# Moving a per-layer embedding's projection to the front of a one-core decoder-layer kernel, with its norm applied at the last gate

## The chip, the cores and the metric

The kernel runs on one core of a Trainium2 chip. The metric is the device time of one execution in microseconds; each kernel is run several times and the median is compared. PE is the matrix engine (TensorE), DVE VectorE, ACT ScalarE, POOL GpSimd, and SP (SyncE) issues most DMAs.

## The reference

One decoder layer on 1024 tokens of width 1024, all in fp32. The part that the change touches is the per-layer embedding `e`; everything else comes before or after it.

```
u = rmsnorm(h, mix_norm_w); proj = u @ w_in             # gated DeltaNet and latent attention read proj
h = h + concat(y_gdn, y_mla) @ w_out
h = h + square(relu(rmsnorm(h, mlp_norm_w) @ w_up)) @ w_down
e = rmsnorm(p @ w_ple_proj, ple_post_norm_w)            # p: 1024 x 256, w_ple_proj: 256 x 1024
gate = sigmoid(rmsnorm(h, ple_gate_norm_w) @ w_ple_gate)
h = h + gate * e
return rmsnorm(h, final_norm_w)
```

`e` needs only `p` and weights, none of the layer's other results. It is used in the last step alone.

## The kernel before

The 1024 tokens are 8 blocks of 128 rows. Every fp32 product is three matmuls on fp32r halves (`three`, L212: hi by hi, hi by lo, lo by hi), so each operand is split into a high part (a cast on ACT) and a low part (a subtraction on DVE or POOL). A weight is loaded, cast and split by `load_rows` (L195 on).

The work up to the MLP is cut into named steps. The table `STEPS` (L65 to 92) lists their names in the order in which they are written out; a loop runs them. A scheduler then orders the instructions of each engine; it starts from that order. Each engine and each DMA queue goes through its instructions in order, so a DMA on SP's queue waits for those in front of it. SBUF is a set of 4 KB-a-row slots in five pools (`SLOTS`: u 16, m 8, g 14, w 7, r 3), and `HOMES` says from which pool a named tile takes its slot. PSUM banks are shared out by `TAGS`.

The steps at the front are:

- `ldx{b}` loads a block of x (512 KB, SP), `nx{b}` squares its rows (ACT), takes the root (POOL) and scales it (DVE, L175); `tx{g}_{k}` transposes the blocks of a token group (PE `pt_x`, L188) and splits them into `uT`.
- `ldm{k}` loads a quarter of the misc weights (the columns for gates and latents), `spm{k}` splits it into `mwh`, `mwl`; `misc{b}` multiplies one block by all four quarters, 24 matmuls into `acc_m` of 432 columns.
- `wl{m}` loads a column block of the input weights; `ip{m}` multiplies it (`acc_p`, L233 to 236). `ip4` is the first. It needs all of `uT`.

The embedding's steps are `plew` (loads the row of norm weights `rowp` and the weights `wp0`, `wp1`, and splits them), `ei{b}` (loads a 128 x 256 block of p into `et`, two transposes `pt_e`, split into `pthl`) and `eo{b}` (12 matmuls of 512 columns into two banks `pe`; per bank a copy on ACT to `et` and a Square on ACT whose sum goes to `se`; POOL makes the root; DVE scales by it and by `rowp`, L1218; SP stores the block to `ep_d`). They stand in the middle of the attention's steps (`s`, `v`, `ve` and others), between `vc0` and `s13`.

After the steps come the MLP's up and down stages, and the gate stage (L1541 to 1593). There `gate_in(b)` normalises block b of h by `norm_rows` (ACT, POOL, DVE) into `xg`, transposes it (`pt_g`) and splits it into `gh`, `gl`; it is called one block ahead. 48 matmuls `pgt` a block follow, the sigmoid `sg`, the product with `et` loaded from `ep_d`, the sum into `hb` and the final norm.

Of the kernel before, what the change touches and what calls it, by code (L numbers as in the profile page):

```python
# [70 lines left out]
sub sub0 ssq1_1 sub1 la11 sub2 sub3 sub4 sub5 sub6 sub7 sub8 sub9 xout ssq1_0 cv2 ssq2_1 wl8 wl9 ssq2_0 ip3 cv3 wl13
qout0 ip8 la10 cv8 rv0_0 rv0_1 kbd1_0 ga3 ga2 ssq3_0 qout1 wl11 ip9 cv9 kbd3_0 kbd2_0 tl0 kbd0_1 ga1 ga0 tm0 ip11
tn0 ip10 wl12 kbd1_1 rv1_0 tl1 tm1 kbd0_0 mw0 cv10 tl2 tl3 ip12 cv12 tn1 mw1 kbd3_1 kbd2_1 ssq3_1 rv2_0 rv1_1 tm2
tn2 cv11 ip13 cv13 rv3_1 tm3 tn3 mw2 mw3 rv3_0 mu0 sc0 rv2_1 mu3 mu1 wl15 mu2 sc1 sc2 sc3 wl14 ip15 qout2 ip14 cv14
la01 lt0_2 sc4 lt1_1 lt0_0 sc5 cv15 lt0_1 sc6 lt1_0 sc7 sc8 sc9 sc10 wv0 vb1 wpe qp0 vb0 qp1 sc11 vb3 rq8 vb2 lt1_2
rkey sc12 sc13 sc14 qout3 ol6 qp7 qr00 qp2 vb6 wn0 kn0_1 vb5 ol0 vb4 kn0_0 sc15 ol2 ol3 qn0_0 qp4 vb7 ol1 kp3 oa0
qp5 oa1 kp0 ob0 qp6 qp3 qn0_1 qr01 qr11 oa2 ro0_0 s0_1 qr10 s0_2 s0_3 ro0_1 s0_0 v0_0 v0_1 v0_2 s1_2 s1_0 s1_1 v0_3
ve0 s1_3 v1_0 v1_1 v1_2 v1_3 v1_4 kp1 s2_0 v1_5 kp2 v1_6 v1_7 ve1 ob1 ob2 s2_2 oa3 s2_1 ol4 oa4 ob3 s2_3 ob4 s3_1
ol5 s3_0 oa6 v2_0 s3_3 v2_1 v2_2 oa5 ob6 s3_2 v2_3 wn1 qn1_0 ro1_0 qn1_1 kn1_1 ve2 v3_0 v3_1 kn1_0 ro1_1 v3_2 v3_3
v3_4 s4_2 s4_1 fa0 ol7 s4_0 oa7 s5_2 s4_3 v3_5 v3_6 v3_7 ve3 v4_0 v4_1 v4_2 s5_1 fb0 s5_0 s6_2 s5_3 v4_3 ob5 s6_1  # L80
ve4 v5_0 kp5 s7_1 v5_1 v5_2 v5_3 v5_4 v5_5 v5_6 wv1 vc1 s6_3 ob7 ro2_0 s7_2 v5_7 s7_0 vc0 plew ei0 ei1 eo1 eo0 s6_0
h2 ve5 v6_0 v6_1 v6_2 wn2 kn2_0 v6_3 vc4 vc5 vc3 s7_3 vc7 ve6 v7_0 v7_1 v7_2 v7_3 qn2_0 vc6 vc2 v7_4 fa1 ei2 v7_5
qn2_1 kp4 s8_3 kn2_1 s8_1 eo2 ro2_1 v7_6 s8_2 s8_0 kp7 s9_3 s10_3 s9_1 s9_0 v7_7 ve7 v8_0 fb1 v8_1 v8_2 v8_3 s9_2
ve8 v9_0 v9_1 v9_2 v9_3 v9_4 ei3 s10_0 eo3 s10_2 s10_1 s11_1 s11_0 ei4 v9_5 v9_6 v9_7 ro3_0 ve9 s11_2 eo4 v10_0
v10_1 v10_2 v10_3 ve10 s11_3 ei5 ro3_1 eo5 wn3 qn3_0 kn3_0 v11_0 kn3_1 kp6 v11_1 v11_2 v11_3 v11_4 fa2 s12_2 qn3_1
# [1537 lines left out]
```

## Time and profile before

| | |
|---|---|
| time, three runs | 1462.49, 1461.21, 1453.26 us; median 1461.21 |
| profiled execution | 1459.25 us, of which 1457.5 are the span from the first to the last instruction |
| mean granted PE clock | 0.972 |
| busy share of the span | PE 95%, DVE 69%, ACT 45%, POOL 21% |
| first matmul of the input projection (`ip4`) | 69.38 us from the span's start |
| the embedding's steps | 485 to 612 us |
| gate stage | 1350 us to the end |

All durations come from the profiled execution; the times of the runs come without a profile. Rows give the engine, the line of the kernel, the operation and the tiles (out<-in, without buffer numbers). In rows by stretch the columns are the busy time and count of PE, PEld (weight loads), DVE, ACT and POOL, then PE's clock, the share of the DMA engines and GB/s.

### The profile page before, as it was taken

To read this page: it belongs to the slowest core of one execution; us is meant where nothing else is said; L and a number is where in the kernel's file an instruction comes from. 1 tells how busy PE (TensorE), PEld (TensorE's weight loads), DVE (VectorE), ACT (ScalarE), POOL (GpSimd) and SP (SyncE) were. 2 spreads that over 40 slices of the span, in tenths; PEclk is the share of its full clock that TensorE was granted. 3 is DMA by queue.
4 is the path that set the end of the run, shared out by engine and by line. 5 is a ranking of instruction groups with operands and counts; after the bars stand their busy time and mean duration, and the time that the engine had idled before them with its cause. 6 is when DMAs were issued, how large, how long until landed. Compare 5 with 4: busy or idle time off the path is not lost.

```text
span 1457.5 us, 22314 instructions
## 1 busy us (share of the span) xinstructions
PE 1380.4 (95%) x8575; PEld 1130.7 (78%) x8575; DVE 1007.5 (69%) x1617; ACT 662.8 (45%) x1169; POOL 307.4 (21%) x417
## 2 busy tenths in 40 slices
PE   5999968999899999999989999999999999999897
...
GB/s 214 49 54 59 131 58 130 85 81 86 59 66 65 140 82 106 152 196 130 88 66 151 159 159 159 159 137 125 214 333 230 159 96 126 183 116 134 170 44 58
DMA packets 133590, 182.54 MB, mean 125 GB/s; under 512 B 38896, under 2 KB 88188, under 8 KB 133484
## 3 DMA queue, kind: packets, MB, share of 16 engines
...
q10 hardware_dynamic: 160, 0.27, 0.0%
...
## 4 chain that ended last, share of the span: by engine, by line
PE 47%; DVE 11%; DMA 8%; ACT 6%; issue 3%; POOL 1%; SPq 1%; DVEq 0%; POOLq 0%; ACTq 0%
DMA i_d<-D 4%; PE dmo L214 3%; PE dme L214 3%; PE dmo L215 3%; PE dme L215 3%; PE dme L213 3%; PE dmo L213 3%; DMA dar<-i_d 2%; PE pgt L215 2%; PE pgt L213 2%; PE pgt L214 2%; PE um L215 2%; PE um L214 2%; PE um L213 2%; PE pt_p L1119 1%
## 5 line engine op out<-in xcount | busy, mean ns | idle before, releaser
L1495 DVE TENSOR_TENSOR dal<-dar,dah 128x1024 fp32r<-128x1024 f32 x56 | 68.5, 1224 | 74.4 <-issue 32.1
L1544 POOL DMA_DIRECT2D rowg<-in_ple_gate_norm_w x1 | 0.6, 644 | 505.4 <-DVE dbs L1499 505.4
L214 PE MATMUL dme<-dbl,dah 128*128 128x512 f32 x256 | 99.7, 390 | 0.0
L215 PE MATMUL dme<-dbh,dal 128*128 128x512 f32 x256 | 99.4, 390 | 0.0
L213 PE MATMUL dme<-dbh,dah 128*128 128x512 f32 x256 | 99.2, 390 | 0.0
L1494 ACT CAST dah<-dar 128x1024 fp32r<-128x1024 f32 x56 | 58.8, 1050 | 62.0 <-DMA dar<-i_d 59.5
L1501 ACT CAST dbh<-dbs 128x1024 fp32r<-128x1024 f32 x40 | 42.1, 1053 | 90.1 <-DVE dbs L1499 45.6
L214 PE MATMUL dmo<-dbl,dah 128*128 128x512 f32 x192 | 74.4, 390 | 1.8 <-DVE dbl L1502 1.8
L215 PE MATMUL dmo<-dbh,dal 128*128 128x512 f32 x192 | 74.3, 390 | 0.0
L213 PE MATMUL dmo<-dbh,dah 128*128 128x512 f32 x192 | 72.8, 390 | 0.0
L180 DVE TENSOR_TENSOR phl<-pt_p,phl 128x512 fp32r<-128x512 f32 (+1 forms) x96 | 51.8, 550 | 17.8 <-ACT phl L179 16.8
L1098 DVE TENSOR_REDUCE stat<-ps_s 128x1 f32<-128x384 f32 (+5 forms) x96 | 51.5, 551 | 16.4 <-PE ps_s L1097 9.7
L213 PEld LDWEIGHTS dme<-dbh,dah 128*128 128x128 f32 x256 | 48.1, 188 | 10.0
L214 PEld LDWEIGHTS dme<-dbl,dah 128*128 128x128 f32 x256 | 48.1, 188 | 9.9
L215 PEld LDWEIGHTS dme<-dbh,dal 128*128 128x128 f32 x256 | 48.1, 188 | 9.9
L213 PE MATMUL um<-uc,t52h 128*128 128x512 f32 x128 | 51.4, 402 | 3.5 <-DVE Cb L1420 2.7
L179 ACT CAST phl<-pt_p 128x512 fp32r<-128x512 f32 (+1 forms) x96 | 44.5, 480 | 21.9 <-PE pt_p L1119 19.5
L1502 DVE TENSOR_TENSOR dbl<-dbs,dbh 128x1024 fp32r<-128x1024 f32 x40 | 48.9, 1222 | 6.7 <-ACT dbh L1501 6.4
L214 PE MATMUL um<-uc,t52h 128*128 128x512 f32 x128 | 50.8, 397 | 2.6 <-DVE uc L1282 2.6
L214 PE MATMUL um<-uc,t34h 128*128 128x512 f32 x128 | 50.7, 396 | 0.7 <-DVE uc L1282 0.7
L213 PE MATMUL um<-uc,t34h 128*128 128x512 f32 x128 | 50.9, 398 | 0.0
L215 PE MATMUL um<-uc,t34l 128*128 128x512 f32 x128 | 50.4, 393 | 0.0
...
## 6 DMA issues: line engine op xcount, KB each, us to landing
dar<-i_d SPq DMA_DIRECT2D x56, 512.0 KB, 3.8
...
wu<-in_w_up SPq DMA_DIRECT2D x32, 512.0 KB, 4.7
x<-in_x SPq DMA_DIRECT2D x8, 512.0 KB, 9.8
h<-in_x SPq DMA_DIRECT2D x8, 512.0 KB, 4.5
ep_d<-et SPq DMA_DIRECT2D x8, 512.0 KB, 2.8
yr<-y_d SPq DMA_DIRECT2D x8, 512.0 KB, 5.8
h_d<-h SPq DMA_DIRECT2D x8, 512.0 KB, 2.6
```

The lines of the kernel that those rows point to most:

```text
L179: nc.scalar.copy(out=hi, in_=src)
L180: nc.vector.tensor_tensor(out=lo, in0=src, in1=f(hi), op=ALU.subtract)
L213: nc.tensor.matmul(outp, ah, bh, start=first, stop=False)
L214: nc.tensor.matmul(outp, ah, bl, start=False, stop=False)
L215: nc.tensor.matmul(outp, al, bh, start=False, stop=last)
L1098: nc.vector.tensor_reduce(out=st[:, c:c + 1], in_=ps[c], axis=AX.X, op=ALU.max, negate=True)
L1119: nc.tensor.transpose(pt[:, i * P:(i + 1) * P], pn_view(u, i)[:, kb * P:(kb + 1) * P], ident)
L1494: nc.scalar.copy(out=ah, in_=raw)
L1495: nc.vector.tensor_tensor(out=al, in0=raw, in1=f(ah), op=ALU.subtract)
L1501: nc.scalar.copy(out=bh, in_=s_)
L1502: nc.vector.tensor_tensor(out=bl, in0=s_, in1=f(bh), op=ALU.subtract)
L1544: nc.gpsimd.dma_start(out=rowg, in_=ple_gate_norm_w[0].partition_broadcast(P))
```

## The change

- `plew`, `ei{b}`, `eo{b}` move from the attention to the front of `STEPS`, among the loads of x and of the misc weights. The order of these front steps is another one too, and a few later steps change places (`la10`, `wl13`, `wl15`, `kp0`, `kp5`, `kp7`, `xout` and some near the end of the attention).
- p comes in two loads of four blocks each (`lp0`, `lp1`, new tiles `pb0`, `pb1`) in place of eight. Two blocks share a `pthl` tile.
- `eo{b}` stores the product as it is: one bank is copied by ACT, the other by DVE; the two Squares, the root and the scaling are gone. `ep_d` becomes eight tensors, one a block.
- In the gate stage, `gate_in(b)` loads the block of `ep_d`, and `norm_rows` normalises it with `rowp` into `en`. `rowp` is loaded at the start of this stage.
- Tiles change pools: the weights `wp0`, `wp1` to w, `pthl` to u, `x1`, `x2` to u.

```
-ldx0 ldm0 start ldx2 ldx1 ldx7 ldx3 ldm1 mixcol ldm2 nx0 nx1 ldm3 ldx5 tx0_3 nx2 nx3 tx0_7 ldx4 tx0_0 tx0_1 tx1_6
...
+lp0 ldx1 ldx0 plew start ei3 ei0 mixcol nx1 nx0 wl7 ei1 lp1 tx0_7 ei4 eo0
+wl5 ldm1 ldm0 ei2 spm1 eo1 tx0_0 ldx6 tx0_1 tx0_2 wl4 tx0_4 ldx3 masks ldx2 nx3
...
-    ep_d = dr.tile([T, D], F32, name="ep_d")
+    ep_d = [dr.tile([P, D], F32, name=f"ep_d{b}") for b in range(NB)]
...
     def _():
-        ple["row"] = slot("ple", "rowp")
-        nc.gpsimd.dma_start(out=ple["row"], in_=ple_post_norm_w[0].partition_broadcast(P))
         ple["w"] = [load_rows(w_ple_proj, k * P, f"wp{k}", ("plr", "ple", "ple")) for k in range(2)]

+    def ple_load(g):
+        nc.sync.dma_start(out=tile_(f"pb{g}", "pb").rearrange("q (b c) -> q b c", b=4),
+                          in_=p[g * 512:(g + 1) * 512].rearrange("(b q) c -> q b c", q=P))
...
     def ple_in(b):
-        pt_ = tile_(f"pthl{b}", "pth", F32R)
-        pb = tile_(f"et{b}", "et")[:, 0:256]
-        nc.sync.dma_start(out=pb, in_=p[b * P:(b + 1) * P])
-        transpose_split(pp_("pt_e"), [pb[:, 0:P], pb[:, P:2 * P]], pt_[:, 0:256], pt_[:, 256:512])
+        pb = tl[f"pb{b // 4}"][:, b % 4 * 256:(b % 4 + 1) * 256]
+        transpose_split(pp_("pt_e"), [pb[:, 0:P], pb[:, P:2 * P]], *ple_part(b))

     def ple_out(b):
...
-            nc.scalar.copy(out=et[:, hs], in_=pe2)
-            nc.scalar.activation(out=pe2, in_=pe2, func=AF.Square, accum_out=ss[:, h2:h2 + 1])
-        nc.gpsimd.tensor_tensor(out=ss[:, 2:3], in0=ss[:, 0:1], in1=ss[:, 1:2], op=ALU.add)
-        rsqrt_(ss[:, 3:4], ss[:, 2:3], 1.0 / D)
-        nc.vector.scalar_tensor_tensor(out=et, in0=et, scalar=ss[:, 3:4], in1=ple["row"], op0=ALU.mult, op1=ALU.mult)
-        nc.sync.dma_start(out=ep_d[b * P:(b + 1) * P], in_=et)
+            if h2:
+                nc.vector.tensor_copy(out=et[:, hs], in_=pe2)
+            else:
+                nc.scalar.copy(out=et[:, hs], in_=pe2)
+        nc.sync.dma_start(out=ep_d[b], in_=et)
...
+    rowg, rowf, rowp = slot("u", "rowg"), slot("u", "rowf"), slot("m", "rowp")
+    nc.gpsimd.dma_start(out=rowp, in_=ple_post_norm_w[0].partition_broadcast(P))
...
+        ep, et = slot("w", "et5"), slot("g", "en")
+        nc.sync.dma_start(out=ep, in_=ep_d[b])
+        norm_rows(ep, ste[:, b, 0:1], ste[:, b, 1:2], D, rowp, et)
+        return gh, gl, et
```

Three places show how the instructions stand. The first is SP's queue in the first tens of microseconds. Before, it begins with all of x and of the misc weights (`mwr`):

```order
L370 DMA x_128<-in_x 128x1024
L384 DMA mwr_130<-in_w_in 128x2x432
L370 DMA x_137<-in_x 128x1024
L370 DMA x_139<-in_x 128x1024
L370 DMA x_141<-in_x 128x1024
L370 DMA x_143<-in_x 128x1024
L384 DMA mwr_145<-in_w_in 128x2x432
```

In the changed kernel it begins with p and two blocks of x, and goes on like this, from the fourth DMA to the twentieth but one (x_270 is block 6, x_296 and x_317 are blocks 3 and 2, x_363 is block 5; ep_d_77, 78, 80 and 79 are blocks 0, 1, 3 and 2):

```order
L217 DMA w7r<-in_w_in 128x8x128
L395 DMA mwr_233<-in_w_in 128x2x432
L395 DMA mwr_235<-in_w_in 128x2x432
L1232 DMA ep_d_77<-et_209 128x1024
L217 DMA w5r<-in_w_in 128x8x128
L381 DMA x_270<-in_x 128x1024
L1232 DMA ep_d_78<-et_246 128x1024
L381 DMA x_296<-in_x 128x1024
L381 DMA x_317<-in_x 128x1024
L1232 DMA ep_d_80<-et_327 128x1024
L381 DMA x_363<-in_x 128x1024
L395 DMA mwr_375<-in_w_in 128x2x432
```

The loads of x3 and x2 now stand behind the stores of blocks 0 and 1 of the embedding, and that of x5 behind the store of block 3; the store of block 2 follows, and behind it `mwr_387`, x4 and x7.

The second place is PE's row in the front. Before, the misc matmuls of the first blocks begin right behind the transposes of x:

```order
L188 MATMUL pt_x<-ident,x_128 128x128
L188 MATMUL pt_x<-ident,x_139 128x128
L188 MATMUL pt_x<-ident,x_137 128x128
L188 MATMUL pt_x<-ident,x_143 128x128
L213 MATMUL acc_m<-mwh_249,uT_0_189 128x432
L214 MATMUL acc_m<-mwl_250,uT_0_189 128x432
L215 MATMUL acc_m<-mwh_249,uT_0_189 128x432
```

In the changed kernel the projection's blocks 0, 1, 3, 2 and half of 4 stand there with parts of the misc matmuls between them; this is the end of that piece, with the first transposes of x2 and x3 behind it:

```order
L226 MATMUL pe_405<-wp0h,pthl_204 128x512
L224 MATMUL pe_405<-wp1h,pthl_204 128x512
L225 MATMUL pe_405<-wp1l,pthl_204 128x512
L226 MATMUL pe_405<-wp1h,pthl_204 128x512
L199 MATMUL pt_e<-ident,pb_195 128x128 x2
L199 MATMUL pt_x<-ident,x_317 128x128
L199 MATMUL pt_x<-ident,x_296 128x128
L224 MATMUL acc_m<-mwh_365,uT_0_264 128x432
```

All 96 matmuls and 16 transposes of the projection now stand ahead of `ip4`; blocks 4 to 7 stand among the remaining transposes and misc matmuls.

The third place is PE in the attention, where block 1 of the projection stood before among the softmax's transposes (`pt_p`) and the values (`pv`):

```order
L214 MATMUL pv<-wv_5315,cT_0_3382 128x256
L215 MATMUL pv<-wv_5315,cT_0_3382 128x256
L1119 MATMUL pt_p<-ident,pn6a 128x128 x2
L1119 MATMUL pt_p<-ident,pn6b 128x128
L213 MATMUL pe_5435<-wp0h,pthl_5426 128x512
L214 MATMUL pe_5435<-wp0l,pthl_5426 128x512
L215 MATMUL pe_5435<-wp0h,pthl_5426 128x512
L213 MATMUL pe_5435<-wp1h,pthl_5426 128x512
```

In the changed kernel the rows of `pe` are gone from here, and the others follow each other.

More of the change, by code (lines that the diff above doesn't have):

```diff
@@ L71 @@
[L71 to L85, printed above, removed]
@@ new lines @@
+wl5 ldm1 ldm0 ei2 spm1 eo1 tx0_0 ldx6 tx0_1 tx0_2 wl4 tx0_4 ldx3 masks ldx2 nx3
+nx2 eo3 eo2 ldx5 spm0 tx0_6 ldm3 tx0_3 nx5 ldm2 ei5 ldx4 eo4 ldx7 eo5 tx1_7
+tx0_5 nx7 spm3 tx1_1 tx1_5 tx1_2 spm2 tx1_4 columns ei6 nx4 misc0 tx1_3 nx6 eo6 misc1
+tx1_0 tx1_6 tx2_0 tx2_3 misc3 tx2_1 tx2_5 tx2_6 ei7 tx2_2 misc2 eo7 tx2_4 tx2_7 misc5 misc7
+misc6 la00 misc4 ip4 cv4 gates wl6 ip5 cv5 ip7 wl0 ssk1_1 wl1 ssk0_1 ip6 cv7
+dec2 ssk1_0 dec1 ssk0_0 cv6 dec3 wl2 dec0 ssk3_0 ssk2_1 wl10 ssk2_0 gk1 ssk3_1 cvals ip1
@@ new lines @@
+rotary cv1 cunit ip0 cv0 gk0 ssq0_0 ssq0_1 uu1 ip2 gk2 uu2 gk3 uu0 uu3 wl3
+sub sub0 ssq1_1 sub1 la11 sub2 sub3 sub4 sub5 sub6 sub7 sub8 sub9 ssq1_0 cv2 la10
+ssq2_1 wl8 wl9 ssq2_0 wl13 ip3 cv3 xout qout0 ip8 cv8 rv0_0 rv0_1 kbd1_0 ga3 ga2
+ssq3_0 qout1 wl11 ip9 cv9 kbd3_0 kbd2_0 tl0 kbd0_1 ga1 ga0 tm0 ip11 tn0 ip10 kbd1_1
+wl12 wl15 tl1 tm1 cv10 kbd0_0 mw0 rv1_0 tl2 tl3 ip12 tn1 kbd3_1 ssq3_1 kbd2_1 cv12
+mw1 rv2_0 rv1_1 tm2 tn2 cv11 ip13 cv13 tm3 rv3_1 tn3 mw2 mw3 rv3_0 mu0 sc0
+rv2_1 mu3 mu1 mu2 qout2 sc1 sc2 wl14 ip14 ip15 sc3 cv14 la01 lt0_2 cv15 sc4
@@ new lines @@
+lt1_1 rq8 lt0_0 sc5 lt0_1 sc6 lt1_0 sc7 sc8 wv0 vb1 wpe qp0 sc9 vb0 qp1
+sc10 sc11 vb3 vb2 lt1_2 rkey sc12 sc13 qr00 sc14 qout3 ol6 qp7 qp2 vb6 wn0
+kn0_1 vb5 ol0 vb4 kn0_0 sc15 kp0 ol2 ol3 qn0_0 qp4 vb7 ol1 kp3 oa0 qp5
+oa1 ob0 qp6 qp3 qn0_1 qr01 qr11 qr10 ro0_0 s0_1 s0_2 oa2 s0_3 ro0_1 s0_0 v0_0
+v0_1 v0_2 s1_2 s1_0 s1_1 v0_3 ve0 s1_3 v1_0 v1_1 v1_2 v1_3 v1_4 kp1 s2_0 v1_5
+kp2 v1_6 v1_7 ve1 ob1 ob2 s2_2 s2_1 oa3 ol4 oa4 ob3 s2_3 ob4 s3_1 ol5
+s3_0 oa6 v2_0 oa5 v2_1 v2_2 s3_3 v2_3 wn1 ob6 s3_2 qn1_0 ro1_0 qn1_1 kn1_1 ve2
@@ new lines @@
+v3_0 v3_1 kn1_0 ro1_1 v3_2 v3_3 s4_2 s4_1 fa0 ol7 s4_0 v3_4 v3_5 oa7 s5_2 s4_3
+v3_6 v3_7 ve3 v4_0 v4_1 v4_2 s5_1 fb0 s5_0 s6_2 s5_3 kp5 v4_3 s6_1 ve4 v5_0
+ob5 s7_1 v5_1 v5_2 v5_3 v5_4 v5_5 v5_6 wv1 vc1 s6_3 ob7 ro2_0 s7_2 v5_7 s7_0
+vc0 s6_0 h2 ve5 v6_0 v6_1 v6_2 wn2 kn2_0 v6_3 vc4 kp7 vc5 vc3 s7_3 vc7
+ve6 v7_0 qn2_0 v7_1 v7_2 v7_3 vc6 fa1 v7_4 vc2 v7_5 qn2_1 kp4 s8_3 kn2_1 s8_1
+ro2_1 v7_6 s8_2 s8_0 s9_3 s10_3 s9_1 s9_0 v7_7 ve7 fb1 v8_0 v8_1 v8_2 v8_3 s9_2
+ve8 v9_0 v9_1 v9_2 v9_3 v9_4 s10_0 s10_2 s10_1 s11_1 s11_0 v9_5 v9_6 v9_7 ro3_0 ve9
@@ new lines @@
+s11_2 v10_0 v10_1 v10_2 v10_3 ve10 s11_3 wn3 qn3_0 ro3_1 kn3_0 v11_0 v11_1 v11_2 v11_3 v11_4
+fa2 v11_5 kn3_1 kp6 v11_6 v11_7 s12_2 qn3_1 s12_1 s12_0 y0 ve11 s12_3 v12_0 v12_1 v12_2
+v12_3 s13_3 ve12 s13_2 s13_1 fb2 s13_0 v13_0 v13_1 v13_2 s14_1 v13_3 v13_4 y2 v13_5 s14_3
+v13_6 v13_7 s14_2 s14_0 ve13 v14_0 v14_1 y1 v14_2 v14_3 wo0 ve14 s15_0 s15_1 s15_3 s15_2
+wo1 v15_0 h6 v15_1 wo2 wo3 y4 y5 y3 fa3 v15_2 v15_3 v15_4 v15_5 h3 v15_6
+h4 pa4 h7 pa6 y6 v15_7 ve15 fb3 h0 wo4 h5 pa7 wo7 wo5 y7 rsy
@@ L92 @@
+pa5 wo6 pa2 h1 pa3 pa0 wu0 pb3 pb2 nh2 nh3 pa1 pb0 uo0 pb5 pb7
+pb1 nh0 nh1 th0_1 pb4 nh7 wu1 nh4 nh5 pb6 nh6 th0_0 th0_2 th1_2 th0_3 th1_1
+th1_0 th1_3
 """
```

31 lines of the change are left out of this document (12 added, 19 removed), and 10 rows, old and new, of the table HOMES.

## The prediction

> **What bounds the kernel now.** I read the page first: the share of each engine, then PE's busy tenths in 40 slices.
>
> ```profile
> span 1457.5 us, 22314 instructions
> PE 1380.4 (95%) x8575; PEld 1130.7 (78%) x8575; DVE 1007.5 (69%) x1617; ACT 662.8 (45%) x1169; POOL 307.4 (21%) x417
> ...
> PE   5999968999899999999989999999999999999897
> ```
>
> PE is busy for 95% of the span, so most work taken from PE shortens the kernel and most work added lengthens it. The exceptions are the slices with a low PE digit; the first (0 to 36 us) has 5. The change takes PE work out of slices 14 to 17, where the digit is 9 throughout, and puts it into that first slice. So I asked next for busy time by stretch (us, then each engine's busy time and count): the front, a stretch before the projection, and the one that holds it.
>
> ```profile
> 0.00:10.00 10.00, 1.39 (x5) 0.90 (x5) 1.81 (x2) 3.51 (x5) 7.78 (x35) 1.00 0.77 238
> 10.00:20.00 10.00, 4.51 (x16) 3.02 (x17) 5.59 (x9) 7.60 (x15) 2.90 (x6) 1.00 1.01 378
> 20.00:30.00 10.00, 10.00 (x44) 8.72 (x44) 7.77 (x18) 9.52 (x20) 7.59 (x9) 1.00 0.43 112
> 30.00:40.00 10.00, 7.70 (x42) 5.94 (x40) 9.76 (x30) 3.69 (x5) 5.27 (x4) 1.00 0.18 54
> 60.00:70.00 10.00, 10.00 (x53) 9.61 (x52) 2.50 (x9) 3.81 (x15) 5.45 (x21) 1.00 0.08 31
> 480.00:625.00 145.00, 136.68 (x838) 111.66 (x837) 111.16 (x223) 119.07 (x310) 39.38 (x51) 0.99 0.40 133
> 450.00:480.00 30.00, 28.58 (x282) 22.75 (x280) 27.64 (x54) 22.81 (x61) 13.53 (x24) 1.00 0.19 54
> 850.00:950.00 100.00, 99.74 (x439) 81.91 (x438) 76.65 (x109) 47.41 (x61) 0.00 (x0) 1.00 0.44 145
> ```
>
> The stretch of the projection has PE busy 94% (136.68 of 145). The one before it has 95% without any of the projection. So PE sets the pace in both.
>
> A matmul's own row overstates its cost, since neighbours overlap. Starts tell it:
>
> ```profile
> 19.27 0.73 PE L213 MATMUL acc_m<-mwh,uT 128*128 128x432 f32 x1 [0.60 <-DVE uT L183]
> ...
> 24.53 0.56 PE L215 MATMUL acc_m<-mwh,uT 128*128 128x432 f32 x1
> 24.89 0.41 PE L213 MATMUL acc_m<-mwh,uT 128*128 128x432 f32 x1
> ...
> 25.64 0.38 PE L188 MATMUL pt_x<-ident,x 128*128 128x128 f32 x2
> ...
> 69.00 0.36 PE L214 MATMUL acc_m<-mwl,uT 128*128 128x432 f32 x1
> 69.19 0.35 PE L215 MATMUL acc_m<-mwh,uT 128*128 128x432 f32 x1
> 69.38 0.39 PE L233 MATMUL acc_p<-uT,w4h 128*128 128x512 f32 x1
> 69.61 0.40 PE L234 MATMUL acc_p<-uT,w4h 128*128 128x512 f32 x1
> ```
>
> Three readings. The front ends at 69.38, when ip4 (L233, the first matmul of the input projection) starts. A warm 432-column matmul costs 0.19 (69.00 to 69.19) and a 512-column one about 0.23; over 850 to 950 it is 100/439 = 0.228 at most, and I use 0.226, as a few records are missing. Two transposes take 0.38 together and 0.27 alone, 0.1 from start to start. Until 24.89 the 432-column matmul took 0.36.
>
> **What leaves the attention stretch.** The first row is all work on the tile pe (the projection's sums) in this stretch, the second on pt_e (its transposes); then groups of instructions, the softmax's split phl for comparison.
>
> ```profile
> 480.00:625.00 145.00, 26.52 (x96) 17.45 (x96) 18.98 (x48) 0.99 0.40 133
> 480.00:625.00 145.00, 3.23 (x16) 1.91 (x16) 3.32 (x8) 3.04 (x8) 0.99 0.40 133
> L1218 DVE SCALAR_TENSOR_TENSOR et<-et,se,rowp 128x1024 f32<-128x1024 f32 x8 | 10.2, 1279 | 1.3 <-POOL se L150 1.2
> L1214 ACT COPY et<-pe x16: 576/586/603, 503.1 to 608.1; 128x512 f32<-128x512 f32 x16
> L180 DVE TENSOR_TENSOR phl<-pt_p,phl 128x512 fp32r<-128x512 f32 (+3 forms) x63 | 34.1, 550 | 13.3 <-ACT phl L179 12.5
> L193 POOL TENSOR_TENSOR wp0l<-wp0r,wp0h 128x1024 fp32r<-128x1024 f32 x1 | 2.4, 2369 | 0.5 <-ACT wp0h L192 0.5
> L192 ACT CAST wp0h<-wp0r 128x1024 fp32r<-128x1024 f32 x1 | 1.0, 1048 | 1.0 <-DMA wp0r<-in_w_ple_proj 1.0
> ```
>
> PE: 96 x 0.226 = 21.7, and 16 transposes at 0.1 = 1.6, together **23.3 us**. Upper bound: the modelled rows, 26.52 without transposes, overlap counted twice. ACT loses 18.98 + 3.04 + two casts of 1.05 = 24.1, DVE 3.32 + 10.2 = 13.5, POOL two splits and the small norm operations. What remains, 95 us of ACT and 97.6 of DVE, in 145 - 23 = 122 us would load ACT to 78% and DVE to 80%; the row of 450 to 480 shows DVE at 92% (27.64 of 30) with PE still at 95%. So the next limit is not reached: I take **-23**, bounds -12 (half of it only filled waits of the softmax chain) and -26.5.
>
> **What the front gains.** Work before ip4 now: 192 acc_m matmuls x 0.195 = 37.4 and 64 transposes pt_x at 0.1 = 6.4, about 44 of 69.4 us. So 25 us of PE's front is waiting, or the slow rate until 24.89; 23.3 would just fit if every hole could be filled. It can't: the holes lie before 25 us, and data sets when work can start.
>
> ```profile
> 4.13 1.06 ACT L173 ACTIVATE dump<-x 128x1024 f32<-128x1024 f32 x1 [0.34 <-DMA x<-in_x]
> ...
> 5.09 0.19 ACT L173 ACTIVATION_READ_ACCUMULATOR dump<-x 128x1 f32 x1
> ...
> 5.58 0.19 POOL L148 TENSOR_SCALAR rsx<-ssx 128x1 f32<-128x1 f32 x1
> ...
> 7.43 0.59 POOL L150 TENSOR_TENSOR rsx<-rsx,half_neg 128x1 f32<-128x1 f32 x1
> ...
> 8.05 0.75 DVE L175 TENSOR_SCALAR x<-x,rsx 128x1024 f32<-128x1024 f32 x1 [0.71 <-POOL rsx L150]
> 8.86 0.72 PEld L188 LDWEIGHTS pt_x<-ident,x 128*128 128x128 f32 x4 [5.37 <-DVE x L175]
> ...
> 13.91 1.06 ACT L173 ACTIVATE dump<-x 128x1024 f32<-128x1024 f32 x1 [0.39 <-DMA x<-in_x]
> ...
> h<-in_x SPq DMA_DIRECT2D x8, 512.0 KB, 4.5
> ```
>
> In the changed order the queue of SP holds stores of projected rows between the loads: ep_d of block 1 stands ahead of the loads of x3 and x2, that of block 3 ahead of x5 and a quarter of the misc weights, that of block 2 ahead of the last quarter, x4 and x7. A load behind a store is issued only when the store's data are there. Before, x3 was in at 13.9 (the row at 13.91). Step by step:
>
> 1. wp0r is fourth in the queue, behind 1.5 MB; at 238 to 378 GB/s shared with what follows, it lands at about 11. Cast 1.05, POOL split 2.37, then the split of wp1 2.4: wp1l is there at about 17.3. Block 0 is projected by 18.5 and block 1, twelve matmuls partly at the slow rate, by 22.5. Evacuated (0.59) and stored: 23.4.
> 2. x3 and x2 are issued by 24.4 and land 4.5 later, 29. Two squares with their read-outs on ACT (2 x 1.25), POOL's two operations (0.75) and the scaling (0.75): x2 is usable at about 32.5.
> 3. PE has work until then: blocks 3, 2 and half of 4 of the projection, parts of the misc matmuls. Done before that point: about 54 matmuls of the projection and its transposes (12.2 + 1.4), twelve acc_m (2.3) and 14 pt_x (1.4), 17.3 of the 67.3 us. Left: 50. 32.5 + 50 = 82.5, and with 1 to 4 us for waits behind ACT's strict order (the square of x5, which waits for its load, stands ahead of two casts and a scale that PE wants) ip4 starts at 83.5 to 86.
>
> I take 84.5: **+15**. Lower bound +8 (block 1 stored 5 earlier, no waits), upper bound +38 (second rival). From ip4 the order is nearly the old one and PE is full (row 60 to 70), so the shift passes on undiminished.
>
> The slow rate ended at 24.89, 5.6 us after steady work had begun (the first misc matmul starts at 19.27); in the changed order steady work begins at about 14.8, so the fast rate should come by 20.4, and PE's idle time to 32 is small. If it came only at 32, the 9.1 us of work between 22.5 and 32 would take 9.1 x 0.36/0.195 = 16.8, a further +7.
>
> The Trainium skill, "TensorE: Matmul & The Clock Gate", Part 1: The HAM clock gate, says that a PE left idle falls to half rate and gets full rate after some 3.4 us of sustained work; by that rule work moved into a front that waits for data may run at half rate, where in the attention it ran at full rate. The rows agree on the two rates (0.36 against 0.195); whether PE falls back after it has risen, no row of the front shows. By the rule the sum would be the same if PE's idle times stay short, and 7 us longer if not.
>
> **The gate stage.** Per block it gains a square on ACT, two POOL operations and a scaling on DVE:
>
> ```profile
> L168 DVE SCALAR_TENSOR_TENSOR xg<-hb,stg,rowg 128x1024 f32<-128x1024 f32 x7 | 9.0, 1284 | 7.4 <-POOL stg L150 7.3
> 1350.00:1400.00 50.00, 46.34 (x223) 38.10 (x222) 25.86 (x34) 22.02 (x37) 16.89 (x21) 1.00 0.36 133
> L213 PE MATMUL pgt<-wg0h,gh 128*128 128x512 f32 (+1 forms) x17 | 6.8, 399 | 3.3 <-ACT gh L179 3.3
> 1357.64 2.40 POOL L193 TENSOR_TENSOR wg7l<-wg7r,wg7h 128x1024 fp32r<-128x1024 f32 x1
> ...
> 1360.98 1.29 DVE L168 SCALAR_TENSOR_TENSOR xg<-hb,stg,rowg 128x1024 f32<-128x1024 f32 x1 [5.51 <-POOL stg L150]
> 1364.96 1.09 ACT L1577 ACTIVATE sg<-pgt 128x512 f32<-128x512 f32 x2 [7.02 <-PE pgt L215]
> ```
>
> A block holds 48 x 0.226 + 0.8 = 11.7 us of PE. DVE is busy for 52% of 1350 to 1400 and ACT for 44%; 1.3 more in 11.7 adds 11% to each, so PE covers them. The one tight place is the second block: its xg waits on POOL behind the eight weight splits (to 1360.0), and the new norm's operations go in front: 0.75 on POOL and 1.28 on DVE, so xg, ready at 1362.3 now, is ready at 1364.3; PE comes to it about when its first half block ends, before 1364.96, where the sigmoid starts. I take **+1.5**, bounds 0 and +4 (about half of a 1.3 for each of 7 blocks). The row weight's broadcast load comes from POOL ahead of the splits; it waits for a buffer that PE leaves some 96 matmuls before the stage, 96 x 0.226 = 22 us. The eight splits, 2.4 each, end at 1360 and so begin after that.
>
> The sum: 15 - 23 + 1.5 = **-6.5**, on the profiled execution's own 1459.25 (span 1457.5 and 1.75 around it): **1452.8 us**. The median of the runs, 1461.21, is 2 higher, and the runs lie between 1453.26 and 1462.49; a difference of 1% (14.6 us) is about what a measurement of this kernel can tell from none.
>
> **Rivals.**
>
> 1. *The front hides it.* The 25 us of holes take most of the projection: blocks 0 to 3 done before 25 us, stores early, ip4 at 75 to 79 (+6 to +9). For: PE has 25 us to spare in the first 69. Against: the weights' casts and splits must end first (17.3 at the earliest, with POOL's 2.4 each), and the holes lie mostly before 20. Time: 8 - 24 + 0 = -16, 1443. Chance 0.2.
> 2. *The stores on SP's queue make the front serial* (slower). Place: SP, three round trips: store of block 1, then x3 and x2; store of block 3, then x5; store of block 2, then the last misc weights, x4 and x7. One trip is 0.7 (issues) + 4.5 (landing) + 2.75 (norm) + 2.7 (twelve matmuls) + 0.6 = 11.3. One is in my sum; if the other two are not covered by PE's other work, or the slow rate stays, ip4 comes 22.6 later, at 107: 37.6 - 23 + 1.5 = +16, 1475. It decides the sign from ip4 after 91 (no gain), and measurably from 105.5. Against: the loads wait for different blocks that PE does in one row. Chance 0.13.
> 3. *The projection was filler.* DVE waits 12.5 us for ACT's copies of the softmax's transposes (row of phl), so that chain sets a part of the pace; half of the 23.2 comes back as PE waits: 15 - 12 + 1.5 = +4.5, 1463.8. Against: 95% without it in 450 to 480. Chance 0.15.
> 4. *The norm doesn't leave the path*: per gate block 1.3 more, 8 x 1.3 = 10.4 in place of 1.5: 1461.7. Against: the 3.3 us of waits that pgt shows in all. Chance 0.03.
>
> The forecast itself has 0.49. Faster by over 1% is the first rival and the low edge of the forecast, 0.25; slower by over 1% is the second, 0.13; within 1%, 0.62. The range: the forecast with its bounds is 1446 to 1460; to leave out no more than 2 in 10 it takes in most of the first rival and the third and the lower half of the second, 1441 to 1472.
>
> **What would show it.** ip4's first matmul at 83 to 86 (75 to 79 by rival 1, over 95 by rival 2); x3's square at about 29; the stretch between the start of the first s6 step and the same later step shorter by 23 with PE's share unchanged (rival 3: share down to about 87%); gate blocks still 11.7 us apart. The forecast is wrong if the matmuls of the front stay at 0.36 or more beyond 30 us, or if a DMA of the front lands more than 3 us after its time above.

## The result and the profile after

| | before | after |
|---|---|---|
| median of the runs | 1460.18 us (4 runs, 1453.26 to 1462.49) | 1478.74 us (4 runs, 1474.52 to 1482.42) |
| ratio, 95% interval | | 1.0126 [1.0083, 1.0169] |
| profiled execution, span | 1459.25, 1457.5 us | 1474.52, 1472.5 us |

The changed kernel is slower by 1.3%, and the interval leaves no room for a gain; 1452.8 was forecast, 25.9 us less. The page of the changed kernel, its shares and its slices:

```profile
span 1472.5 us, 22272 instructions
PE 1388.7 (94%) x8575; PEld 1133.3 (77%) x8575; DVE 1016.8 (69%) x1625; ACT 663.8 (45%) x1148; POOL 312.8 (21%) x409
...
PE   7998987999989988999989999999999999999897
```

PE's first slice rose from 5 to 7: the projection did fill some of the front. PE is busy for 8 us longer (1388.7 against 1380.4) with the same 8575 matmuls, a first sign that they ran slower somewhere.

Cutting both traces at the same instructions shows where the 15.0 us of the span lie. The columns are those of the rows by stretch: busy time and count of PE, PEld, DVE, ACT, POOL, then PE's clock. Before, four stretches: from `ip4` to the 385th `acc_p` matmul (input projection), from the last `pk` to the first `ps_s` (inverse and scan; `ps_s` are the softmax's scores), from the 49th `po_a` (the attention's output sums) to the last `ps_s` (the attention, with the projection in it), and the gate stage:

```profile
69.38:176.37 106.99, 106.99 (x714) 85.30 (x714) 68.16 (x117) 41.80 (x66) 23.24 (x16) 1.00 0.32 83
242.48:404.06 161.58, 153.84 (x2045) 124.13 (x2045) 95.89 (x276) 47.53 (x95) 47.84 (x56) 0.91 0.33 86
478.69:613.41 134.72, 127.13 (x781) 103.73 (x780) 104.49 (x211) 109.54 (x290) 32.63 (x48) 0.99 0.35 111
1350.20:1457.50 107.30, 95.54 (x473) 79.99 (x471) 52.06 (x70) 39.63 (x72) 25.00 (x37) 0.97 0.23 86
```

The same stretches of the changed kernel:

```profile
84.81:199.25 114.44, 109.10 (x714) 86.05 (x714) 70.37 (x121) 47.07 (x76) 29.85 (x31) 0.97 0.31 79
265.81:426.02 160.21, 152.00 (x2045) 122.84 (x2045) 93.79 (x276) 47.82 (x95) 46.89 (x56) 0.93 0.33 87
498.50:623.25 124.75, 111.37 (x668) 88.97 (x668) 93.91 (x194) 86.93 (x231) 18.16 (x20) 0.93 0.27 82
1361.01:1472.50 111.49, 98.58 (x473) 82.16 (x471) 61.60 (x78) 48.29 (x88) 36.36 (x53) 0.95 0.22 83
```

| stretch | forecast | measured |
|---|---|---|
| front, to `ip4` | +15 | +15.4 (84.81 - 69.38) |
| input projection, from `ip4` on | 0 | **+7.4** (114.44 - 106.99) |
| scan and what lies up to the attention | 0 | -3.1 (the second row gives -1.4) |
| attention | -23 | **-10.0** (124.75 - 134.72) |
| from the last `ps_s` to the gate stage (end of the attention, MLP) | 0 | +1.0 |
| gate stage | +1.5 | **+4.2** (111.49 - 107.30) |
| sum | -6.5 | +15.0 |

The list of moved steps under The change is too short: behind `ip4` the steps `gates`, `ssk`, `dec` and `wl6` change places too, and the second row of the table is about them. The front came as worked out. Three terms did not, and the attention's is the largest. There the row shows it at once: PE lost 15.8 us of busy time, not 23.3, its idle time rose from 7.6 to 13.4, and its clock fell from 0.99 to 0.93.

### The profile page after: what moved, and what is told of

It reads as the page before. It is cut to its first block, busy times and chain, and to the rows that moved or that the text cites. A ratio compares the mean times of both kernels' runs of the same rounds, so it can differ in the third digit from the quotient of the medians.

```text
span 1472.5 us, 22272 instructions
## 1 busy us (share of the span) xinstructions
PE 1388.7 (94%) x8575; PEld 1133.3 (77%) x8575; DVE 1016.8 (69%) x1625; ACT 663.8 (45%) x1148; POOL 312.8 (21%) x409
## 4 chain that ended last, share of the span: by engine, by line
PE 38%; DVE 8%; DMA 4%; ACT 3%; issue 2%; SPq 0%; POOL 0%; DVEq 0%; POOLq 0%; ACTq 0%
PE dme L224 4%; PE dme L225 4%; PE dme L226 4%; DMA i_d<-D 4%; PE dmo L225 3%; PE dmo L226 3%; PE dmo L224 3%; PE um L225 2%; PE um L226 2%; PE um L224 2%; PE pgt L226 2%; PE pgt L224 2%; PE pgt L225 2%; DVE D L1455 1%; PE po_o L226 1%
```

## The experiments

Theory A: a part of the projection's matmuls had filled waits of the softmax chain, and they had kept PE's clock up; without them PE waits more and runs slower. Theory B: all of the 23 us left, and something of the new order gave it back. The stretches below are cut as above; each median comes with its ratio to the kernel before in the same session.

### What the projection cost in the attention

**e2_no_projection**: the kernel before without the embedding's steps; its gate stage reads rows of x in place of the embedding.

```
-vc0 plew ei0 ei1 eo1 eo0 s6_0
+vc0 s6_0
...
-        nc.sync.dma_start(out=et, in_=ep_d[bs])
+        nc.sync.dma_start(out=et, in_=x[bs])
```

> The kernel before with the embedding's projection left out altogether (steps plew, ei, eo; the gate stage loads rows of x in place of e, so that its loads and its work stay). It measures what the projection cost in its old place, with nothing added elsewhere. Theory A (half of it filled waits of PE in the softmax's chains, and the idle time that it leaves also brings half-clock windows): the stretch from 478 to 720 us gets 10 to 13 us shorter, PE's share in it falls to about 89%, total about 1447. Theory B (it cost its full 23.3 us there; the rest was lost to the other steps that changed places in the attention): 22 to 24 shorter with PE's share still 94%, total about 1436.

Measured: 1449.01 us, ratio 0.9905 [0.9872, 0.9937]: 12.9 us under the kernel before beside it (1461.88).

**e8_matmuls_alone**: e2 with 96 bare matmuls of 128x512 where the projection's had stood.

```
+            for k in range(6):
+                nc.tensor.matmul(pe2, dm, dm.unsqueeze(1).to_broadcast([P, 4, P]), start=k == 0, stop=k == 5)
```

> The kernel before without the projection, but with 96 matmuls of 512 columns on a constant tile put where the projection's stood (results unused; the gate stage loads rows of x in place of e). It adds 21.7 us of PE work and nothing on ACT, DVE or the queues to the run without projection. Theory A (half of PE's work there fills waits): the stretch from 478 to 720 is 8 to 12 longer than without the projection, total about 1458 to 1460. Theory B (PE sets the pace fully, the rest of the gain was lost elsewhere): 20 to 22 longer, total about 1470. Theory C (the projection's price in its old place is that of its work on ACT and DVE): less than 4 longer, 1452.

Measured: 1462.64 us (10 runs), ratio 1.0020 [0.9994, 1.0046]; 13.6 over e2, or 16.2 when each is taken against the kernel before of its own session (1459.28 and 1461.88).

**e12_after_plus_matmuls**: the changed kernel with the same bare matmuls, at the projection's old places (steps `fl0` to `fl7`, 12 matmuls each).

```
-vc0 s6_0 h2 ve5 v6_0
+vc0 fl0 fl1 s6_0 h2 ve5 v6_0
...
```

> The changed kernel with 96 matmuls of 128x512 (21.7 us of PE, results unused) put back into the attention where the projection stood; its transposes, casts, evacuations and norms stay away. The theory: the projection's matmuls there had filled PE's waits and kept its clock up, so the bare matmuls cost less than their own time: the stretch from the first po_a to the last ps_s grows by 9 to 14 us over the changed kernel's, its half clock falls from 17 us to below 12 and its idle time from 13 to below 10; the whole 1488 to 1493. The rival, that PE sets the pace there: the stretch grows by 20 to 23 us, the whole 1498 to 1502.

Measured: 1486.13 us, ratio 1.0194 [1.0139, 1.0249], 7.4 over the changed kernel. The attention's row in e2, in e8 and in e12:

```profile
481.25:603.73 122.48, 107.46 (x658) 85.92 (x658) 91.51 (x191) 84.74 (x226) 18.14 (x20) 0.96 0.27 82
```

```profile
474.25:610.38 136.13, 127.24 (x756) 104.51 (x755) 93.51 (x194) 86.48 (x230) 18.11 (x20) 0.95 0.24 75
```

```profile
501.74:634.71 132.97, 123.17 (x765) 100.77 (x764) 94.32 (x195) 87.86 (x234) 18.13 (x20) 1.00 0.26 80
```

Without the projection the stretch is 12.2 shorter than before; the bare matmuls, 21.7 us of PE work, bring back 13.7 in the one order and 8.2 in the other. In e12 the idle time fell from 13.4 to 9.8 and the clock rose from 0.93 to 1.00. Theory A holds against B in both orders, in e12 more strongly than expected (8.2 where 9 to 14 were); the projection's casts, copies and norm cost the attention next to nothing.

The expectations of e2 and e8 speak of a longer stretch, to about 720 us. Cut at the first `um` matmul, the MLP's first, it is in the kernel before, in e2 and in e8:

```profile
478.69:716.48 237.79, 229.47 (x1278) 188.98 (x1277) 163.63 (x296) 151.65 (x364) 62.12 (x76) 0.99 0.39 132
```

```profile
481.25:713.27 232.02, 213.07 (x1166) 172.76 (x1166) 153.77 (x280) 129.54 (x307) 49.92 (x49) 0.98 0.32 106
```

```profile
474.25:717.90 243.65, 232.25 (x1261) 191.26 (x1261) 153.39 (x280) 130.14 (x306) 49.08 (x49) 0.97 0.31 100
```

There e2 is only 5.8 shorter than before, where 10 to 13 were expected, and e8 is 11.6 longer than e2. So half of what e2 gains up to the last `ps_s` is lost again before the MLP in this execution; both figures are far from the 20 and more of theory B.

**e4_norm_at_gate_only**: the kernel before, projection in its old place, but stored unnormalised and normalised at the gate as in the changed kernel.

```
-            nc.scalar.activation(out=pe2, in_=pe2, func=AF.Square, accum_out=ss[:, h2:h2 + 1])
...
-        nc.vector.scalar_tensor_tensor(out=et, in0=et, scalar=ss[:, 3:4], in1=ple["row"], op0=ALU.mult, op1=ALU.mult)
...
+        norm_rows(ep, ste[:, b, 0:1], ste[:, b, 1:2], D, rowp, et)
```

> The kernel before with the projection in its old place, but stored unnormalised (one half copied by ACT, one by DVE) and normalised in the gate stage as in the changed kernel. It takes 13.5 us of DVE less 5.5 for the copies and 14 us of ACT out of the attention and leaves PE's work there. Theory A (PE and the chains behind it set the pace there, ACT and DVE are not the limit): the attention changes by less than 3 us, the gate stage gets 3 to 5 longer, total about 1461 to 1464. Rival (ACT's and DVE's share of the projection is what cost time): the attention gets 8 to 12 shorter and the total is about 1452.

Measured: 1473.25 us (10 runs), ratio 1.0084 [1.0057, 1.0111]; neither theory's total (1461 to 1464, and 1452) came. Its rows for attention and gate stage:

```profile
474.64:613.72 139.08, 129.80 (x781) 106.06 (x781) 102.65 (x211) 95.89 (x250) 22.69 (x22) 0.96 0.33 106
1354.22:1465.30 111.08, 97.14 (x473) 81.06 (x471) 61.57 (x78) 48.44 (x89) 36.46 (x53) 0.97 0.23 85
```

ACT's load in the attention fell by 13.7 us and nothing was gained (139.08 against 134.72); the gate stage paid 3.8. So the norm's move alone is a loss of about 11 us by the medians, of which the gate's 3.8 are explained. The profile, of the fastest of the ten runs, shows 4.4 more in the attention; what the rest is stays open.

### The wait behind ip4

PE's waits in that stretch of the changed kernel (us in total, times, longest), then from its timeline two rows of POOL and DVE and one of PE (start, duration, line, operation, and the idle time before it with its releaser):

```profile
PE pe L493 <- DVE R L488: 4.9, 1, 4.9
```

```profile
137.79 2.29 POOL L488 TENSOR_TENSOR R<-m,g_t 128x1024 f32<-128x1024 f32 x1
138.23 2.92 DVE L488 TENSOR_TENSOR R<-m,g_t 128x1024 f32<-128x1024 f32 x1
141.21 5.33 PE L493 MATMUL pe<-R,striL 128*128 128x512 f32 x6 [4.91 <-DVE R L488]
```

The steps `dec0` to `dec3` (the decays) build a tile `R` and multiply it by a triangle of ones. PE stood at one of them for 4.9 us until `R` came from DVE, which took 2.92 us beside POOL's; then its six matmuls ran at half rate. Two rows by stretch show the fall: clock 0.50 in the five microseconds after the wait, before which PE was idle for 4.

```profile
135.00:140.00 5.00, 0.87 (x5) 0.42 (x4) 3.93 (x6) 3.52 (x8) 4.57 (x2) 0.94 0.00 0
140.00:145.00 5.00, 3.79 (x5) 1.73 (x6) 5.00 (x6) 0.60 (x1) 0.08 (x1) 0.50 0.00 0
```

**e1_gates_first**: the changed kernel with `gates`, which computes the decays' inputs, ahead of `ip4`, as before.

```
-misc6 la00 misc4 ip4 cv4 gates wl6
+misc6 la00 misc4 gates ip4 cv4 wl6
```

> The changed kernel with one step moved: `gates` stands again ahead of `ip4 cv4`, as before the change. Theory (the changed order put the gates' chain of small DVE operations behind the first convolutions, so the decay matmuls waited and PE stood still at 135 to 141): ip4 stays at 84.8, pg comes at about 100 in place of 119.5, the wait of PE for R (4.9 us) and the half clock behind it go, the shift against before at 150 us falls from +23 to about +16, and the kernel takes about 7 us less, 1467. Rival (the shift at 150 comes from the weights w6, w1, w2 that are loaded and split late): pg comes early, but PE waits for weights instead, and the time stays within 2 us of 1474.

Measured: 1480.72 us, ratio 1.0122 [1.0090, 1.0155]; the wait stayed though the gates came first. The first theory on it fell.

```profile
PE pe L493 <- DVE R L488: 5.2, 1, 5.2
```

**e7_after_no_projection**: the changed kernel without the projection; the gate stage normalises rows of x instead.

```
-lp0 ldx1 ldx0 plew start ei3 ei0 mixcol nx1 nx0 wl7 ei1 lp1 tx0_7 ei4 eo0
+ldx1 ldx0 start mixcol nx1 nx0 wl7 tx0_7
...
-        nc.sync.dma_start(out=ep, in_=ep_d[b])
+        nc.sync.dma_start(out=ep, in_=x[b * P:(b + 1) * P])
```

> The changed kernel with the projection left out (steps lp, plew, ei, eo; the gate stage loads rows of x in place of e and norms them). The order of all other steps is that of the changed kernel. Theory (the front's 15.4 us is PE's added work, not the order): ip4 starts at 69 to 71; the wait for the decays at 125 to 130 stays if it is the order's, so the total is about 15 below the changed kernel: 1459 to 1462. Rival (the new order of the loads is itself worse): ip4 at 75 or later.

Measured: 1471.06 us (6 runs), ratio 1.0075 [1.0036, 1.0114], where 1459 to 1462 was expected. `ip4` starts at 70.77, 1.4 later than before: 14.0 of the front's 15.4 are the projection, the other order there is nearly free. The wait for `R` is still there (5.2), so it doesn't come from the projection.

```profile
PE pe L491 <- DVE R L486: 5.2, 1, 5.2
```

**e5_decays_early**: the changed kernel with `gates`, the `dec` and `ssk` steps and the `ip` between them in their order of before.

```
-misc4 ip4 cv4 gates wl6 ip5 cv5 ip7 wl0 ssk1_1 wl1 ssk0_1 ip6 cv7 dec2 ssk1_0 dec1 ssk0_0 cv6 dec3 wl2 dec0 ssk3_0
+misc4 gates ip4 cv4 ssk0_0 ssk0_1 ip5 dec0 dec1 cv5 wl0 ssk1_1 wl6 ip7 ssk1_0 wl1 ip6 cv7 dec3 wl2 ssk3_0 dec2 cv6
```

> The changed kernel with the steps from `ip4` to `ssk3_0` in the order that they had before the change: the decays `dec0` and `dec1` stand again behind `ip5`, not behind `ip6`. Theory (the wait of 5 us at 141 and the half clock around it are from the decays' place: PE comes to their matmuls when everything ahead of them is done and DVE and POOL still build R side by side): the wait goes, the shift against before at 150 us falls from +23 to +15 or +17, about 1467 in all. Rival (the slots that the projection's weights hold until 71 us delay the later weights, whatever the order): PE waits elsewhere in 85 to 150 and the shift stays above +20.

Measured: 1480.36 us, ratio 1.0139 [1.0091, 1.0187]. The stretch is what it was before, with no idle time:

```profile
85.06:191.97 106.91, 106.91 (x714) 85.26 (x714) 68.72 (x121) 43.09 (x73) 27.91 (x23) 1.00 0.35 89
258.75:427.34 168.59, 160.41 (x2053) 129.35 (x2054) 95.55 (x278) 48.86 (x98) 48.56 (x61) 0.87 0.33 86
501.16:633.31 132.15, 116.33 (x669) 93.12 (x668) 93.87 (x194) 86.77 (x231) 18.12 (x20) 0.88 0.26 78
```

So the order of these steps is the cause of the +7.4, and the wait's row names the decays; e1 shows that the place of `gates` alone is not it. Yet the median did not fall: in the profile, of the slowest of the four runs (1489.09), the scan (second row) is 8.4 and the attention (third) 7.4 longer than in the changed kernel, at clocks of 0.87 and 0.88. That made the clock the next question.

### The gate stage

**e3_no_gate_norm**: the changed kernel, stored rows used without their norm.

```
-        norm_rows(ep, ste[:, b, 0:1], ste[:, b, 1:2], D, rowp, et)
```

> The changed kernel without the norm in the gate stage (the stored rows are used as they are; the load stays in gate_in). Theory (the added square, root and scaling delay the next block's xg on POOL and DVE): the gate stage, 4.6 us longer than before, comes back to its old length, 1470. Rival (the stage is longer because two half-clock windows fell into it, whatever is in it): it stays at +3 or more.

Measured: 1477.03 us, ratio 1.0093 [1.0061, 1.0125].

**e6_late_norm_too**: e5, and the norm of block b written behind the `xg` of block b + 1.

```
-        norm_rows(ep, ste[:, b, 0:1], ste[:, b, 1:2], D, rowp, et)
-        return gh, gl, et
+        return gh, gl, ep
...
+        et = slot("g", "en")
+        norm_rows(ep, ste[:, b, 0:1], ste[:, b, 1:2], D, rowp, et)
```

> The kernel of the run above, and in the gate stage the embedding's norm of a block is written out behind the next block's xg, not ahead of it. Theory (the gate stage lost 4.6 us because ste and en stood ahead of stg and xg of the second block on POOL and DVE): the gate stage falls back to at most 1 us over its old length; with the decays' 7 us this takes 11 us off the changed kernel: about 1463, level with the kernel before. Rival (any added work on DVE in this stage costs, since PE's half clocks follow): the stage keeps +3 or more.

Measured: 1477.23 us, ratio 1.0113 [1.0072, 1.0155]. The gate stage in e3 and in e6:

```profile
1362.51:1470.20 107.69, 96.94 (x473) 81.00 (x471) 52.04 (x70) 39.67 (x73) 25.12 (x37) 0.96 0.23 86
```

```profile
1365.08:1472.80 107.72, 95.22 (x473) 80.01 (x471) 61.43 (x78) 47.55 (x88) 35.28 (x53) 0.99 0.23 88
```

Both have before's 107.3 within half a microsecond, and e6 does so with the whole norm in it (DVE 61.43). So the work of the norm costs next to nothing there; its place ahead of `xg` does. Neither median shows it (1477.03 and 1477.23 against 1478.74). Of the seven profiles with the norm in that place, six have this stage 3.7 to 4.3 longer than before; the seventh, e12, has it 0.1 shorter. The three without it or with it behind `xg` (e3, e6, e11) have +0.3 to +1.1.

### The clock in the scan

The clock's record in all fourteen profiles changes only on a grid of 3.413 us, whose phase differs from run to run. I counted each window's matmul work (columns, by the share of the array in use) as a share of the window: a 128x128 matmul of 512 columns counts a 16th, 0.213 us, near the 0.23 between the starts of two such; one of 64 columns on 64x64 counts a 32nd of that. Then I asked whether the next window was at half rate. Windows ahead of the record's first entry (at 15 to 25 us) are not counted:

| work in a full-rate window | windows | next at half rate | | work in a half-rate window | windows | next at half rate |
|---|---|---|---|---|---|---|
| under 0.2 | 130 | 72% | | under 0.2 | 123 | 95% |
| 0.2 to 0.3 | 154 | 29% | | 0.2 to 0.3 | 70 | 77% |
| 0.3 to 0.4 | 231 | 8% | | 0.3 to 0.4 | 93 | 44% |
| 0.4 and more | 5062 | 0% (one) | | 0.4 and more | 75 | 3% |

The one exception counts a matmul that starts at the window's very end. By the rows' times PE was at least 95% busy in 17 of the 157 windows that half rate followed. One of them, and the window behind it, in the attention of the kernel before; 16 of its 29 matmuls have a single column:

```profile
598.40:601.81 3.41, 3.41 (x29) 3.27 (x29) 3.23 (x8) 3.36 (x8) 0.00 (x0) 1.00 0.00 0
601.81:605.22 3.41, 3.41 (x12) 2.82 (x11) 0.74 (x3) 1.74 (x6) 2.37 (x2) 0.50 0.74 244
```

The scan is made of 64x64 matmuls, so its windows hold little work though PE is busy. To test it, **e9_before_fill**, **e10_after_fill** and **e11_late_norm_fill** are the kernel before, the changed kernel and e6 with extra matmuls into the unused half of the scan's banks.

```
+                for g_ in pgt_:
+                    for k in range(2):
+                        nc.tensor.matmul(g_[:, 256:512], dm, dm.unsqueeze(1).to_broadcast([P, 2, P]), start=True, stop=True)
                 for pr in prs:
```

> The kernel before, with 120 extra matmuls of 128x256 (results unused) in the scan over the chunks: two into the unused half of each bank pgr, ahead of the chunk's own small matmuls, 0.85 us of PE per chunk at full rate, 12.8 us in all. The theory: the half clock in the scan (27.5 us of the stage from the end of um to the first ps_s in the profile of before, in windows whose matmuls fill under 0.35 of the array's time) comes from too little work in the window ahead. It expects the half clock of that stage to fall below 10 us, the stage to change by -6 to +2 us although PE gets 12.8 us of work more, and the whole by the same. The rival, that the half clock there comes from something else (a limit of power, a random draw), expects 20 to 45 us of half clock as before and the stage longer by 6 to 13 us, 1467 to 1474.

> The changed kernel with the same extra matmuls. Theory: half clock of the scan's stage from 23.8 below 10 us, its runs closer together than the 7.9 us over which those of the changed kernel lie, the whole 1470 to 1480. Rival: half clock unchanged, 1484 to 1492.

> The changed kernel with the decays earlier, the gate's norm written behind the next block's xg, and the same extra matmuls. In the profiles the two moves took 7.5 and 3.7 us out of their stages, yet the medians (1477.2 against 1478.7) did not show it. If the scan's half clock, which differs from run to run, hid it, this kernel is 8 to 12 us below the changed kernel with the extra matmuls alone. If the moved steps cost as much elsewhere, the two are within 4 us.

Measured: 1471.55 us (ratio 1.0086 [1.0053, 1.0119]), 1492.86 (1.0233 [1.0201, 1.0264]) and 1487.55 (1.0187 [1.0154, 1.0220]). The scan from 345 to 402 us in the kernel before, then in e9, and a row that shows what the extra matmuls cost:

```profile
345.00:402.00 57.00, 50.34 (x544) 40.43 (x544) 39.09 (x127) 16.10 (x43) 12.97 (x26) 0.78 0.26 71
```

```profile
345.00:402.00 57.00, 56.57 (x607) 45.34 (x605) 34.23 (x114) 13.88 (x37) 11.21 (x24) 1.00 0.28 80
```

```profile
350.70 0.48 PE L831 MATMUL pgr<-dm 128*128 128x256 f32 x2
351.11 0.44 PE L835 MATMUL pgr<-S,W 64*64 64x64 f32 x4
```

The clock did what the theory says: between the last `pk` and the first `ps_s` 27.5 us at half rate became 4.3 in e9, and 23.8 became 6.5 in e10. The time did not follow: e9's stretch grew by 6.5 us where -6 to +2 was expected, and e10 took 1492.86 where 1470 to 1480 was. The runs came closer together in e9 only: its four lie within 2.1 us, where seven of the kernel before spread over 10.7, but those of e10 and e11 spread over 5.9 and 6.4, though e11's profile has no half rate in the scan at all. A pair of extra matmuls takes 0.41 us from start to start (350.70 to 351.11), twice my price, and the 60 pairs cost 25 us, more than the full rate gives back (about half of 23.2 us). Padding is no way to win here. e11 against e10 shows 5.3 us of the 11 that the decays and the late norm save in their stretches (8 to 12 expected if the scan's clock had hidden all of it, under 4 if the moves cost as much elsewhere): between the two. What holds back the rest is open.

## Why the prediction was wrong

**The front: right.** The block-1 store was forecast at 23.4 and x3's square at 29, x2 usable at 32.5 (its scaling ends at 33.3), `ip4` between 83.5 and 86:

```profile
22.91 0.34 SPq L1232 DMA_DIRECT2D ep_d<-et  x1
23.30 1.47 SPq L381 DMA_DIRECT2D x<-in_x  x2
28.98 1.06 ACT L184 ACTIVATE dump<-x 128x1024 f32<-128x1024 f32 x1
...
32.55 0.75 DVE L186 TENSOR_SCALAR x<-x,rsx 128x1024 f32<-128x1024 f32 x1 [0.72 <-POOL rsx L161]
...
84.81 0.39 PE L244 MATMUL acc_p<-uT,w4h 128*128 128x512 f32 x1
```

The fast rate came early enough: the clock's record is at full rate from its first entry, at 16.5 us, to 139.4. The second rival (a front in series) did not occur.

**The attention: the term was mis-sized, and the third rival held in part.** I took -23 from "PE sets the pace in both", a busy share of 95%, and kept -12 as the bound. The changed kernel gained 10.0 there, and e2, in the old order, 12.2. The fourteen profiles, by whether the projection's matmuls (or bare ones) stand in the attention, give:

| | profiles | stretch, mean | PE idle | at half rate |
|---|---|---|---|---|
| matmuls there (before, e4, e8, e9, e12) | 5 | 135.6 us | 8.7 | 6.1 (0 to 13.7) |
| not there (after, e1 to e3, e5 to e7, e10, e11) | 9 | 127.7 us | 14.8 | 22.8 (10.2 to 30.7) |

The difference is 7.9 us. It adds up: 23.3 of work, less 6.1 that came back as waits, less half of the 16.7 us that run at half rate now, 8.3, leaves 8.9. So waits, as the third rival had them, are one part of the loss; the other part is the clock, which none of my cases had for this stretch. Their sizes differ from pair to pair: the kernel before against e2 has 7.4 of waits and 3.4 of clock, e12 against the changed kernel 3.6 and 8.5. Nor were all the waits those of the softmax chain. Of the 5.8 us of idle time that the changed kernel has more, 2.8 are waits for ACT's casts of the weights `wn` and `wv` (0.2 us before), and in e2 3.4 of 7.4:

```profile
PE pv_n L224 <- ACT wn L203: 1.9, 1, 1.9
PE po_a L1135 <- DVE oT L1146: 1.9, 2, 1.2
...
PE pv L224 <- ACT wv L203: 1.1, 1, 1.1
```

A rival stays open beside this: of the nine profiles without the matmuls only e2 has the old order of the other steps, and its stretch is the shortest of the nine (122.48; the others 124.75 to 132.15). Some of the missing gain may be the new order in the attention. The step that failed is the reading of a busy share as "work is worth its time": 23.3 us of work were worth 10.0 in the change and 12.2 in e2. The row of 450 to 480 us, 95% busy without the projection, was no neighbour to argue from: half of its 282 matmuls, 5.7 of its 28.58 us of PE, belong to the scan's outputs. They probably fill the softmax's waits there as the projection does later; no run took them away.

```profile
L875 PE MATMUL pq<-S,zq 64*64 64x64 f32 x80 | 3.4, 224 | 0.8 <-ACT rs__4984 L1146 0.6 <-DVE ot L905 0.3
...
L885 PE MATMUL pav<-Uv,A 64*64 64x64 f32 x64 | 2.3, 221 | 0.0
```

The changed kernel's 111.37 of 124.75 is 89% and e2's 107.46 of 122.48 is 88%, near what the third rival gave as its sign (87%).

The prediction weighed the rule of the Trainium skill ("TensorE: Matmul & The Clock Gate", Part 1: The HAM clock gate) that an idle PE falls to half rate for the front only. There the fall cost nothing; in the attention it cost 3.4 to 8.5 us, by the figures above. The page ties the fall to an idle window; in the attention PE was 89% busy (111.37 of 124.75) and fell all the same.

**From ip4 on: a term left out.** "From ip4 the order is nearly the old one and PE is full, so the shift passes on undiminished" rested on a row that ends at 70 us, 70 us before the wait. The moved names were in the diff; I put at nothing, without a reason, the place of `dec0` and `dec1`, which now stand behind `ip7` and `ip6`, and of the steps around them. It cost 7.4, and e5 shows that it is this order.

**The gate: the mechanism named, the size at its upper bound.** Forecast +1.5 with a bound of +4, measured +4.2. The tight place was the second block, as said; its `xg` was ready at 1374.58, near the forecast 1364.3 shifted by the 10.8 us of the stage's start. What I left out is what PE does behind a wait. PE's waits in this stage, before and after (us, times, longest), and the stretch behind the second block's:

```profile
PE pgt L213 <- ACT gh L179: 3.3, 2, 3.0
PE pgt L215 <- DVE gl L180: 0.4, 1, 0.4
```

```profile
PE pgt L224 <- ACT gh L190: 4.3, 2, 2.6
PE pgt L226 <- DVE gl L191: 1.0, 1, 1.0
```

```profile
1381.00:1386.00 5.00, 4.02 (x12) 3.08 (x12) 4.16 (x5) 2.52 (x6) 3.92 (x6) 0.66 0.00 0
```

The waits grew by 1.6 us only. But behind the waits of the first two blocks a window each ran at half rate (mean clock 0.66 in the row), and with the stage's end the time at half rate rose from 5.8 to 12.1 us: 1.1 of idle time and half of 6.3 make the 4.2. e6 still waits 4.8 us for `gh`, without such a window, and e12 with the changed kernel's own gate stage had none either; so in the changed kernel the waits bring most of the loss by falling into windows of the clock. It is not the only way: e4 lost 3.7 with 2.1 more of idle time and only 1.0 more at half rate.

**The sum.** 15.4 - 7.9 + 7.4 + 4.2, and -2.1 for the other stretches, make 17.0; the medians differ by 18.6, and the profiled execution, at +15.0, drew an attention 2 us better than the mean. The prediction's slower cases each moved one term alone; the attention's bound with the gate's, 15 - 12 + 4 = +7, would have given 1466, inside the range, and it takes the term left out as well to pass its end at 1472.

e2 and e7 split it otherwise: the projection costs 12.9 us where it stood (1461.88 - 1449.01) and in the front 7.7 by the medians (1478.74 - 1471.06), 14.0 by the start of `ip4`. These do not differ by more than the noise, so the move by itself is near no change. The order that came with it, with the norm at the gate, is what cost: e7 and e2 both lack the projection and differ by 22 us. Their profiles differ by 23.3: 6.5 are the decays, 5.3 the gate stage, 7.9 the attention and 3.6 the scan, the last two at lower clocks, and whether the order or chance sets those is not settled. Nor is it why e4, the kernel before with only the norm moved, loses 11 us where the gate stage shows 3.8. No kernel that computes the reference in full beat the one before.
